# Two groups of the second layer's modulation summed on DVE inside the first layer's up-and-down loop

## The chip, the core and the metric

The kernel runs on one core of a Trainium2 chip. The metric is the device time of one execution in microseconds; the time given is the median of several runs. The engines are PE (TensorE, matmul) with its weight loads PEld, DVE (VectorE), ACT (ScalarE), POOL (GpSimd), and SP, which here only issues DMAs.

## What is computed

The reference is a trunk of two layers for two groups of tokens (128 context tokens and 256 sample tokens, width 1024). Cut to what matters here:

```python
def modulation(cond, w, b):
    m = jax.nn.silu(cond) @ w + b            # w is 1024 x 6144
    return jnp.split(m[..., None, :], 6, axis=-1)

def conv_ffn(h, p):
    gate, up = jnp.split(h @ p['ffn_w_up'], 2, axis=-1)
    gate = dwconv3(gate, p['ffn_conv_w'], p['ffn_conv_b'])
    return (jax.nn.silu(gate) * up) @ p['ffn_w_down']

def trunk_layer(x, mod, p, cache):
    shift1, scale1, gate1, shift2, scale2, gate2 = mod
    h = rms_norm(x, p['norm_g'][0]) * (1.0 + scale1) + shift1
    y, ctx_state = token_mixer(h, p, cache)
    x = x + gate1 * rms_norm(y, p['norm_g'][1])
    h = rms_norm(x, p['norm_g'][2]) * (1.0 + scale2) + shift2
    x = x + gate2 * rms_norm(conv_ffn(h, p), p['norm_g'][3])
    return x, ctx_state
```

Each layer's modulation depends only on the two condition vectors (`c_ctx` and `c`), so any of it can be computed at any time before its use. A layer needs `shift1` and `scale1` first, before its mixer; `gate1`, `shift2` and `scale2` behind the mixer; `gate2` behind the FFN.

## The kernel before

All tokens (3 tiles of 128) are worked on together. A layer has four stages: the token projections and the mixer (its instructions in the order in which a scheduler put them), the output projection with the norms (an order written out by hand, `OUT_ORDER`), the loop of the FFN's up and down products (`for f in range(NF)`, NF = 22, scheduler's order), and the FFN's end with the norms and the first projection of the next layer (by hand, `FFN_ORDER`).

**Weights.** Products of f32 weights are made as three products of rounded parts. A weight tile is loaded raw by a DMA on SP's queue, ACT rounds it to `whi` (L355), DVE takes `wlo = raw - whi` (L356), and L380 to L382 or L1243 to L1245 multiply. One step `f` of the FFN loop does 24 matmuls `gps`, 18 `facc` (down products of step f-1, whose inputs `fah`, `fal` are split from `fc` by ACT and DVE), and 24 `ups`. DVE works between: `fc` (L1257, L1258, L1260 for the convolution and the gate, L1492 for the product with `ups`), `fal` and six `wlo`. `gps` and `ups` share a tag of two PSUM banks, "a".

**Modulation.** The class `Ada(l, g)` computes for layer l the group g, two of the six parts of `modulation` (2048 columns). Its 8 steps k (128 rows of `w` each) load two tiles `araw` of 128x1024 f32 (512 KB each) and make four matmuls with the two condition columns padded to 32 (`cs`), L404, which write four 32-row parts of one bank, `adaps`. In the trace one such matmul is two records, so a step is x8. Then `load_end` loads the bias, `end` adds it on DVE (L426 to L437), `columns` transposes four times on PE (`adat`, L443), and `vec` leaves the result in columns. `hold` lays a part sum aside in `sb` (L413) and frees the bank.

**Where the steps run.** Ada(0,0) at the start. In the mixer of layer 0, as side jobs that the scheduler mixes in, Ada(0,1), Ada(0,2) and the first KO = 3 steps of Ada(1,0); its five others as `A0` to `A4` in `OUT_ORDER`, with `as` (bias), `aT` (transposes) and `vc`. The first KF = 5 steps of Ada(1,1) as `A0` to `A4` in `FFN_ORDER`. In the mixer of layer 1, the last three steps of Ada(1,1) and its end, and all eight of Ada(1,2). The FFN loops hold none of them. `idle` (`W0` and so on in the tables) is eight small bf16 products on PE that compute nothing.

**Names.** `fmps` are the mixer's token projections, `sc` an attention's scores, `ptp` the transposes of its probabilities, `hyt`, `hyP`, `hyR` products of the convolution by FFT, `tma`/`tps` the layer 1 projections and the transposes of the norms. `xn` and `x` are the norm's DVE operations (L752, L736), `tmb` a mixer one (L926).

Of the kernel before, what the change touches and what calls it, by code (L numbers as in the profile page):

```python
# [45 lines left out]
ha2 lv2 L4 ia2 A4 u1 U0 as la2 aT G0 G1 U1 vc  # L46
# [11 lines left out]
L4 k1 A4 lv2 la2 k2 hold  # L58
# [210 lines left out]
def trunk(ctx: ExitStack, tc: tile.TileContext, A, O, offs, depth=DEPTH):  # L269
# [46 lines left out]

    cT = per.tile([128, 8, 2], F32, name="cT")
# [67 lines left out]
    class Ada:  # L385
# [53 lines left out]
        def columns(self, tag="n"):  # L439

            self.tp = bank(tag, "adat").rearrange("p (c j x) -> p j c x", c=4, j=4)
            for c in range(4):
                T.transpose(self.tp[:, :, c], self.sb[:, 128 * c:128 * c + 128], ident)  # L443
# [16 lines left out]
    def ada(a, out, k1=8, part=False):  # L460

        for k in range(a.k0, k1):
            a.load(k)
            a.mm(k, last=k1 - 1)
            if k < k1 - 1:
                yield
        if part:
            a.hold(k1)
        else:
            a.load_end()  # L470
            a.end()
            a.columns()
            a.vec(out)
        yield

# [192 lines left out]
    def retention_tables(lgt, pool=None):  # L668
        with (nullcontext(pool) if pool else tc.tile_pool(name="rp", reuse_waits="tile", bufs=1)) as rp:
            kw = [dict(tag="w15", bufs=11)] * 2 if pool else [dict(tag="lag"), dict(tag="tabt")]  # L670
            lag = rp.tile([128, 384], F32, name="lag", **kw[0])
            nc.sync.dma_start(out=lag, in_=A["lag"])
            return rettab(lgt, lambda: rp.tile([128, 384], F32, name="tabt", **kw[1]), lag)
# [594 lines left out]
    KO, KF = 3, 5  # L1268
# [57 lines left out]
    for l in range(depth):  # L1326
# [4 lines left out]
        with ExitStack() as ph:  # L1331
# [11 lines left out]
            jobs = [ada(ahead.pop((l, 1)) if l else Ada(l, 1), vecs), ada(Ada(l, 2), vecs)]  # L1343
            if l + 1 < depth:
                ahead[l + 1, 0] = Ada(l + 1, 0, "r" * (2 * KO + 5) + "hlhlh" + "r" * 6)
                jobs.append(ada(ahead[l + 1, 0], vecs, KO, True))
# [41 lines left out]
            if l == 0:  # L1388
                mkf = hm.tile([128, 256], F32, tag="hm", name="mkf")
                nc.sync.dma_start(out=mkf, in_=A["mask"])  # L1390
                with tc.issue_after(end.ins):
                    V.tensor_copy(maskb, mkf)
                    lps = load_lp(0)
                    rt = retention_tables(lps[2], mx)
# [32 lines left out]
        with ExitStack() as ph:  # L1427
# [30 lines left out]
            if l + 1 < depth:  # L1458
                a = ahead.pop((l + 1, 0))
                for k in range(8 - KO):  # L1460
                    more[f"L{k}"] = lambda k=k: a.load(k + KO)
                    more[f"A{k}"] = lambda k=k: a.mm(k + KO, "a")
                more["as"] = lambda: (a.load_end(), a.end())
                more["aT"] = lambda: a.columns("a")
                more["vc"] = lambda: a.vec(vecs)
# [3 lines left out]
        with ExitStack() as ph:  # L1469
            fx = ph.enter_context(tc.tile_pool(name="fx", reuse_waits="tile", bufs=1))  # L1470
            act, wd = {}, {}
            for f in range(NF):
# [24 lines left out]
                with late if f == 0 else nullcontext():  # L1497
                    wd[f] = wunit(A["wdn"][l, f], 1024, fx, STAG)
                if f == NF - 1:
                    sqrt_table(c[:, 0:1])  # L1500
                if l + 1 < depth:
                    if f == 4:
# [3 lines left out]
                        rt = retention_tables(lps[2])  # L1506
# [23 lines left out]
            if not last:  # L1530
                a1 = ahead[l + 1, 1] = Ada(l + 1, 1)
                for k in range(KF):
                    more[f"L{k}"] = lambda k=k: a1.load(k)
                    more[f"A{k}"] = lambda k=k: a1.mm(k, "m", KF - 1)
                more["hold"] = lambda: a1.hold(KF)
# [36 lines left out]
```

## Time and profile before

| | us |
|---|---|
| median of 3 runs | 1097.02 (1094.13 to 1098.34) |
| the profiled execution | 1093.04 |
| its span, first to last instruction | 1091.2 |
| PE busy in the span | 1072.9 (98%) |
| DVE busy | 658.5 (60%) |
| ACT busy | 504.6 (46%) |
| POOL busy | 62.0 (6%) |
| granted TensorE clock, mean | 0.999 |

The stages in the span: start and mixer of layer 0 to about 258 us, output projection and norms to 303, FFN loop to 556, its end to 592, mixer of layer 1 to about 760, and the output projection, FFN loop and end of layer 1 to 1091. Busy shares are of one engine; the chain of waits follows the work that ended last back to the start, and the time of its pieces is what the span is made of. A run of matmuls overlaps the next one at its end, so a piece of the chain is a little shorter than the run's own duration.

### The profile page before, as it was taken

The page shows a single profiled execution, that of the slowest core. Times are in us where ns is not written, and L with a number is a line of the kernel's source. Part 1 is how long each engine was busy: PE and PEld are TensorE (multiplying, and loading weights), DVE is VectorE, ACT ScalarE, POOL GpSimd, SP SyncE. Part 2 cuts the span into 40 slices and gives each one's busy share as a digit, 9 for nine tenths or more (in the row PEclk, how much of TensorE's full clock was granted, in tenths as well). Part 3 has the DMA queues.
Part 4 walks back from the last instruction along what each step waited for, and adds up shares of the span by engine and source line. Part 5 has one row for each costly group of instructions (what it writes and reads, how often), then busy time and mean ns, then how long its engine had stood idle before and what let it go on. Part 6 is the DMA issues. An engine that isn't in the chain of part 4 may idle for free.

```text
span 1091.2 us, 15755 instructions
## 1 busy us (share of the span) xinstructions
PE 1072.9 (98%) x5843; PEld 892.9 (82%) x5843; DVE 658.5 (60%) x1479; ACT 504.6 (46%) x1105; POOL 62.0 (6%) x74
## 2 busy tenths in 40 slices
PE   9999999999899999999999999999999999999997
PEld 3496767658699999999987786786889999999996
DVE  6868965466785455455565676637676545554544
ACT  6755535235664343344356534542584333434333
POOL 3210000000300000000002000011020000000000
PEclk9999999999999999999999999999999999999999
DMA  9774345866565433333337615461626433343301
GB/s 348 236 264 167 135 150 198 296 213 249 209 218 160 130 121 120 131 117 121 119 111 267 227 61 169 168 233 43 232 69 213 133 127 116 118 141 127 116 20 58
DMA packets 53018, 176.07 MB, mean 161 GB/s; under 512 B 8618, under 2 KB 10538, under 8 KB 52429
## 3 DMA queue, kind: packets, MB, share of 16 engines
q1 hardware_dynamic: 49229, 171.19, 45.5%
q10 hardware_dynamic: 3712, 3.87, 1.0%
q8 instruction: 46, 0.75, 0.3%
q14 instruction: 31, 0.25, 0.1%
HBM read 169.60 MB, written 5.44 MB: 160 GB/s over the span
## 4 chain that ended last, share of the span: by engine, by line
PE 91%; DVE 5%; ACT 1%; issue 1%; DMA 0%; POOL 0%; DVEq 0%; ACTq 0%; POOLq 0%
PE ups L380 6%; PE gps L380 6%; PE ups L382 6%; PE gps L381 6%; PE gps L382 6%; PE ups L381 6%; PE facc L1243 5%; PE facc L1245 5%; PE facc L1244 5%; PE adaps L404 4%; PE fmps L380 4%; PE fmps L382 4%; PE fmps L381 3%; PE acc L1243 2%; PE acc L1244 2%; PE acc L1245 2%
## 5 line engine op out<-in xcount | busy, mean ns | idle before, releaser
L356 DVE TENSOR_TENSOR wlo<-raw,whi 128x512 fp32r<-128x512 f32 (+2 forms) x388 | 254.3, 686 | 220.8 <-ACT whi L355 220.6
L355 ACT CAST whi<-raw 128x512 fp32r<-128x512 f32 (+2 forms) x388 | 221.0, 610 | 276.8 <-PE gps L381 97.1
L1243 PE MATMUL facc<-whi,fah 128*128 128x512 f32 x264 | 104.5, 396 | 0.0
L1244 PE MATMUL facc<-wlo,fah 128*128 128x512 f32 x264 | 104.0, 394 | 0.0
L1245 PE MATMUL facc<-whi,fal 128*128 128x512 f32 x264 | 104.0, 395 | 0.0
L380 PE MATMUL ups<-hTb,whi 128*128 128x386 f32 (+4 forms) x184 | 61.7, 335 | 0.6 <-ACT hTb L772 0.6
L381 PE MATMUL ups<-hTb,whi 128*128 128x386 f32 (+4 forms) x184 | 61.4, 334 | 0.8 <-POOL hTb L775 0.8
L380 PE MATMUL gps<-hTa,whi 128*128 128x386 f32 (+4 forms) x184 | 61.8, 336 | 0.0
L380 PE MATMUL ups<-hTa,whi 128*128 128x386 f32 (+4 forms) x184 | 61.7, 335 | 0.0
L380 PE MATMUL gps<-hTb,whi 128*128 128x386 f32 (+4 forms) x184 | 61.7, 335 | 0.0
L381 PE MATMUL gps<-hTb,whi 128*128 128x386 f32 (+4 forms) x184 | 61.4, 334 | 0.2 <-POOL hTb L775 0.2
L382 PE MATMUL gps<-hTa,wlo 128*128 128x386 f32 (+4 forms) x184 | 61.5, 334 | 0.0
L382 PE MATMUL ups<-hTb,wlo 128*128 128x386 f32 (+4 forms) x184 | 61.5, 334 | 0.0
L382 PE MATMUL ups<-hTa,wlo 128*128 128x386 f32 (+4 forms) x184 | 61.4, 334 | 0.0
L382 PE MATMUL gps<-hTb,wlo 128*128 128x386 f32 (+4 forms) x184 | 61.3, 333 | 0.0
L381 PE MATMUL gps<-hTa,whi 128*128 128x386 f32 (+4 forms) x184 | 61.3, 333 | 0.0
L381 PE MATMUL ups<-hTa,whi 128*128 128x386 f32 (+4 forms) x184 | 61.3, 333 | 0.0
L1245 PEld LDWEIGHTS facc<-whi,fal 128*128 128x128 f32 x264 | 49.6, 188 | 12.1 <-DVE fal L356 0.3
L404 PE MATMUL adaps<-araw,cs 128*32 128x512 f32 x384 | 59.4, 602 | 0.0
L1243 PEld LDWEIGHTS facc<-whi,fah 128*128 128x128 f32 x264 | 49.6, 188 | 10.2 <-ACT fah L355 0.3
L1244 PEld LDWEIGHTS facc<-wlo,fah 128*128 128x128 f32 x264 | 49.6, 188 | 10.0
L1259 ACT ACTIVATE fth<-fc 128x386 f32<-128x386 f32 x44 | 23.2, 528 | 55.1 <-DVE fc L1258 55.0
(367 smaller groups left out, 2319.6 us busy)
## 6 DMA issues: line engine op xcount, KB each, us to landing
araw<-in_ada_dram SPq DMA_DIRECT2D x96, 512.0 KB, 5.1
raw<-in_wup_dram SPq DMA_DIRECT2D x88, 512.0 KB, 3.5
raw<-in_wdn_dram SPq DMA_DIRECT2D x44, 512.0 KB, 3.8
raw<-in_win_dram SPq DMA_DIRECT2D x30, 512.0 KB, 4.3
raw<-in_wout_dram SPq DMA_DIRECT2D x16, 512.0 KB, 5.1
gg<-gd SPq DMA_DIRECT2D x8, 512.0 KB, 6.1
raw<-in_wta_dram SPq DMA_DIRECT2D x8, 416.0 KB, 3.2
x<-in_x_dram SPq DMA_DIRECT2D x6, 512.0 KB
```

The source lines that it names most:

```text
L355: S.copy(hi, src)
L356: (eng or V).tensor_tensor(out=lo, in0=src, in1=hi, op=ALU.subtract)
L380: T.matmul(out, ah, bh, start=start, stop=False)
L381: T.matmul(out, ah, bl, start=False, stop=False)
L382: T.matmul(out, al, bh, start=False, stop=stop)
L404: T.matmul(self.ps[32 * j:32 * j + 32, :], cs[:, k, :], rows[j // 2][:, 512 * (j % 2):512 * (j % 2) + 512], start=(k == self.k0), stop=(k ...
L1243: T.matmul(acc[t][h], ah[:, cs_], wh_[:, hs], start=first, stop=False)
L1244: T.matmul(acc[t][h], ah[:, cs_], wl_[:, hs], start=False, stop=False)
L1245: T.matmul(acc[t][h], al[:, cs_], wh_[:, hs], start=False, stop=last)
L1259: S.activation(out=th, in_=c, func=ACTF.Tanh)
```

## The change

The groups 0 and 2 of layer 1 no longer go over `adaps`. A class `AdaV` loads the same tiles into `avr` (two buffers) and lets DVE multiply each by the condition's value of its row and add it up: `acc` is 128 x 2 conditions x 2048 f32, and each tile takes two DVE operations of 128x1024, `tensor_scalar` for k = 0 and `scalar_tensor_tensor` behind it. When all 16 tiles are in, eight matmuls with a column of ones sum the 128 partitions into a bank of tag "a" (`avps`), and `end`, `columns` and `vec` follow as before. This runs in the FFN loop of layer 0: every step f but 0, 4 and 5 asks twice for the next tile, until both groups are through. So DVE gets 8 operations of `tensor_scalar` and 56 of `scalar_tensor_tensor`, PE 2 x 8 matmuls with ones and 2 x 4 transposes, and SP 32 DMAs of 512 KB in that loop.

Group 1 of layer 1 keeps `adaps`: four steps in `OUT_ORDER`, in place of the five of group 0 (the fifth place becomes `W0`, and `as`, `aT`, `vc` are gone), four in `FFN_ORDER` in place of five (the fifth becomes `W0`; the bias is added there), and only its transposes in the mixer of layer 1. The mixer of layer 0 has no step of layer 1 any more. Of 16 steps that are gone from PE, 3 stood in the mixer of layer 0, 1 in the output stage, 1 in the FFN's end and 11 in the mixer of layer 1. The retention's tables (`lag`, `tab`), which DVE makes at f = 4, lie in the `avr` buffers now.

```diff
 OUT_ORDER:
-ha2 lv2 L4 ia2 A4 u1 U0 as la2 aT G0 G1 U1 vc
+ha2 lv2 ia2 W0 u1 U0 hold la2  G0 G1 U1 
 FFN_ORDER:
-L4 k1 A4 lv2 la2 k2 hold
+ k1 W0 lv2 la2 k2 as
...
+    one = per.tile([128, 34], F32, name="one")
+    V.memset(one, 0.0)
+    V.memset(one[:, 1:2], 1.0)
...
+    def ada_last(a, out):
+        a.columns()
+        a.vec(out)
+        yield
+
+    class AdaV(Ada):
...
+        def rows(self, out):
+            acc = self.pool.tile([128, 2, 2, 1024], F32, tag="avc", name="avc")
+            for k in range(8):
+                for c in range(2):
+                    raw = self.pool.tile([128, 1024], F32, tag="avr", name="avr", bufs=2)
+                    nc.sync.dma_start(out=raw, in_=A["ada"][self.l, 2 * self.g + c, k])
+                    for v in range(2):
+                        sc = cs[:, k, v:v + 1]
+                        if k == 0:
+                            V.tensor_scalar(acc[:, v, c], raw, sc, None, ALU.mult)
+                        else:
+                            V.scalar_tensor_tensor(out=acc[:, v, c], in0=raw, scalar=sc, in1=acc[:, v, c], op0=ALU.mult, op1=ALU.add)
+                    yield
+            self.load_end()
+            ps = self.ps = bank("a", "avps")
+            for v in range(2):
+                for j in range(4):
+                    T.matmul(ps[32 * j:32 * j + 32, :], one[:, 1 - v:33 - v], acc[:, v, j // 2, 512 * (j % 2):512 * (j % 2) + 512],
+                             start=(v == 0), stop=(v == 1))
+            self.end()
+            self.columns(ps)
+            self.vec(out)
+            yield
...
-    KO, KF = 3, 5
+    KO = 4
...
-            jobs = [ada(ahead.pop((l, 1)) if l else Ada(l, 1), vecs), ada(Ada(l, 2), vecs)]
-            if l + 1 < depth:
-                ahead[l + 1, 0] = Ada(l + 1, 0, "r" * (2 * KO + 5) + "hlhlh" + "r" * 6)
-                jobs.append(ada(ahead[l + 1, 0], vecs, KO, True))
+            jobs = [ada_last(ahead.pop((l, 1)), vecs)] if l else [ada(Ada(l, 1), vecs), ada(Ada(l, 2), vecs)]
...
-                a = ahead.pop((l + 1, 0))
-                for k in range(8 - KO):
-                    more[f"L{k}"] = lambda k=k: a.load(k + KO)
-                    more[f"A{k}"] = lambda k=k: a.mm(k + KO, "a")
-                more["as"] = lambda: (a.load_end(), a.end())
-                more["aT"] = lambda: a.columns("a")
-                more["vc"] = lambda: a.vec(vecs)
+                a = ahead[l + 1, 1] = Ada(l + 1, 1, "rrrhlhlh" + "r" * 8)
+                for k in range(KO):
+                    more[f"L{k}"] = lambda k=k: a.load(k)
+                    more[f"A{k}"] = lambda k=k: a.mm(k, "a", KO - 1)
+                more["hold"] = lambda: a.hold(KO)
...
+            avc = tc.tile_pool(name="av", reuse_waits="tile", bufs=1, side="right")
+            av = avc.__enter__()
+            nexts = iter([])
+            if l + 1 < depth:
+                nexts = (s for g in (0, 2) for s in AdaV(l + 1, g, av).rows(vecs))
             for f in range(NF):
...
                     wd[f] = wunit(A["wdn"][l, f], 1024, fx, STAG)
+                if f not in (0, 4, 5):
+                    next(nexts, None)
+                    next(nexts, None)
...
-                        rt = retention_tables(lps[2])
+                        rt = retention_tables(lps[2], av, tag="avr", bufs=2)
+            run(nexts)
+            avc.__exit__(None, None, None)
...
-                a1 = ahead[l + 1, 1] = Ada(l + 1, 1)
-                for k in range(KF):
-                    more[f"L{k}"] = lambda k=k: a1.load(k)
-                    more[f"A{k}"] = lambda k=k: a1.mm(k, "m", KF - 1)
-                more["hold"] = lambda: a1.hold(KF)
+                a1 = ahead[l + 1, 1]
+                for k in range(8 - KO):
+                    more[f"L{k}"] = lambda k=k: a1.load(k + KO)
+                    more[f"A{k}"] = lambda k=k: a1.mm(k + KO, "m")
+                more["as"] = lambda: (a1.load_end(), a1.end())
+                more["W0"] = idle
```

The lines of the changed kernel are moved: L356 is L359 there, L380 to L382 are L383 to L385, L404 is L407, L443 is L446, L885 is L925, L1018 and L1020 are L1058 and L1060, L1257, L1258 and L1260 are L1297, L1298 and L1300, and L1492 is L1533. The DVE sums are L503 and L505, the matmuls with ones L511.

**DVE in the FFN loop.** Before, one step of the loop, from the product with `ups` to the next one:

```order
L1492 TENSOR_TENSOR fc<-ups,fc 128x386
L356 TENSOR_TENSOR wlo<-raw,whi 128x512 x2
L356 TENSOR_TENSOR fal<-fc,fah 128x386
L356 TENSOR_TENSOR wlo<-raw,whi 128x512
L1257 SCALAR_TENSOR_TENSOR fc<-gps,ffh,fc 128x385
L356 TENSOR_TENSOR wlo<-raw,whi 128x512
L1258 SCALAR_TENSOR_TENSOR fc<-gps,ffh,fc 128x385
L1260 SCALAR_TENSOR_TENSOR fc<-fth,fc 128x386
L356 TENSOR_TENSOR wlo<-raw,whi 128x512 x2
```

Now, a step in which the second group is summed, from behind the product with `ups` to before the next one:

```order
L505 SCALAR_TENSOR_TENSOR avc<-avr,cs,avc 128x1024
L359 TENSOR_TENSOR fal<-fc,fah 128x386
L359 TENSOR_TENSOR wlo<-raw,whi 128x512 x2
L505 SCALAR_TENSOR_TENSOR avc<-avr,cs,avc 128x1024
L1297 SCALAR_TENSOR_TENSOR fc<-gps,ffh,fc 128x385
L359 TENSOR_TENSOR wlo<-raw,whi 128x512
L1298 SCALAR_TENSOR_TENSOR fc<-gps,ffh,fc 128x385
L359 TENSOR_TENSOR wlo<-raw,whi 128x512
L505 SCALAR_TENSOR_TENSOR avc<-avr,cs,avc 128x1024
L1300 SCALAR_TENSOR_TENSOR fc<-fth,fc 128x386
L505 SCALAR_TENSOR_TENSOR avc<-avr,cs,avc 128x1024 x2
L359 TENSOR_TENSOR wlo<-raw,whi 128x512
```

Five sums stand between the loop's own operations, here one of them ahead of `fal`. In the whole loop the steps hold 1, 4, 5, 2, 3, 5, 4, 5, 3, then none in three, then 9 (the second group's start, four of them `tensor_scalar`), 5, 5, 5, 5 and 3.

**PE where the first group ends.** After the `ups` of a step, ahead of the next `gps`:

```order
L385 MATMUL ups<-hTb,wlo 128x386
L511 MATMUL avps<-avc,one 32x512 x8
L383 MATMUL gps<-hTa,whi 128x386
L384 MATMUL gps<-hTa,whi 128x386
L385 MATMUL gps<-hTa,wlo 128x386
L383 MATMUL gps<-hTa,whi 128x386
L384 MATMUL gps<-hTa,whi 128x386
L385 MATMUL gps<-hTa,wlo 128x386
L383 MATMUL gps<-hTa,whi 128x386
L384 MATMUL gps<-hTa,whi 128x386
L446 MATMUL avps<-cst_79,avs 128x128 x4
L385 MATMUL gps<-hTa,wlo 128x386
```

The matmuls with ones and the transposes stand in PE's row of weight products, eight `gps` apart; the second group's are 14 apart.

**PE in the mixer of layer 1.** Before, behind a block of attention scores:

```order
L1018 MATMUL sc<-gqk 128x384
L1020 LDWEIGHTS identb
L1020 MATMUL sc<-maskb,identb 128x128
L404 MATMUL adaps<-araw,cs 32x512 x3
L380 MATMUL fmps<-hTa,whi 128x386
L381 MATMUL fmps<-hTa,whi 128x386
L382 MATMUL fmps<-hTa,wlo 128x386
```

Now, at the same place:

```order
L1058 MATMUL sc<-gqk 128x384
L1060 LDWEIGHTS identb
L1060 MATMUL sc<-maskb,identb 128x128
L385 MATMUL fmps<-hTb,wlo 128x386
L383 MATMUL fmps<-hTb,whi 128x386
L384 MATMUL fmps<-hTb,whi 128x386
L385 MATMUL fmps<-hTb,wlo 128x386
```

Until the transposes `ptp` of these scores' probabilities there stood `adaps` x3, 24 `fmps`, `adaps` x4 and 2 `fmps`; now 26 `fmps`.

## Rows read from the trace of the kernel before

**Rows 1.** The page: span, busy time by engine, chain that ended last.

```profile
span 1091.2 us, 15755 instructions
PE 1072.9 (98%) x5843; PEld 892.9 (82%) x5843; DVE 658.5 (60%) x1479; ACT 504.6 (46%) x1105; POOL 62.0 (6%) x74
PE 91%; DVE 5%; ACT 1%; issue 1%; DMA 0%; POOL 0%; DVEq 0%; ACTq 0%; POOLq 0%
```

**Rows 2.** Busy time by stretch: length, engines, granted clock, DMA share, GB/s.

```profile
306.00:556.00 250.00, 250.00 (x1309) 235.15 (x1308) 138.18 (x245) 102.72 (x191) 0.33 (x2) 1.00 0.42 134
592.00:720.00 128.00, 128.00 (x751) 97.63 (x750) 79.01 (x207) 60.46 (x162) 5.09 (x7) 1.00 0.48 173
650.00:700.00 50.00, 50.00 (x324) 34.70 (x323) 34.28 (x93) 23.69 (x67) 0.00 (x0) 1.00 0.50 169
403.16:415.84 12.68, 12.68 (x68) 11.88 (x67) 6.45 (x11) 4.94 (x10) 0.00 (x0) 1.00 0.38 124
```

**Rows 3.** Chain of waits, 612 to 716 us (mixer, layer 1): shares, one piece.

```profile
by line: PE fmps L380 15.4%; PE fmps L382 14.5%; PE fmps L381 14.1%; PE adaps L404 12.3%; PE pv L890 8.4%; PE ptp L885 6.9%; PE sc L1018 6.5%; PE sc L976 6.4%; PE uqps L965 5.0%; DMA raw<-in_win_dram 4.7%; PE uvps L958 1.9%; PE ukps L952 1.
673.59 0.99 PE adaps L404 x6
```

**Rows 4.** PE's own row: start, duration, line, operation, records.

```profile
720.14 1.07 PE L404 MATMUL adaps<-araw,cs 128*32 128x512 f32 x8
680.42 0.82 PE L885 MATMUL ptp<-cst,P 128*128 128x128 f32 x6
205.43 1.92 PE L404 MATMUL adaps<-araw,cs 128*32 128x512 f32 x16
796.12 0.61 PE L1278 MATMUL wps<-identb 128*128 128x128 bf16 x8
407.68 0.39 PE L1245 MATMUL facc<-whi,fal 128*128 128x512 f32 x1
```

**Rows 5.** Chain of waits, 212 to 224 us (end of layer 0's mixer): shares.

```profile
by line: PE adaps L404 47.6%; PE fmps L382 14.6%; PE fmps L380 10.3%; PE fmps L381 10.2%; PE hyR L1062 8.7%; PE hyP L1086 5.2%; PE hyP L1085 5.2%; PE hyI L1063 3.6%
```

**Rows 6.** Chain of waits, pieces in the output stage and in the FFN's end.

```profile
292.95 0.99 PE adaps L404 x8
296.88 0.46 PE adat L443 x4
...
583.93 0.99 PE adaps L404 x8
```

**Rows 7.** What PE waited for, 600 to 800 us: total, times, longest.

```profile
PE hyF L1104 <- POOL Y L1078: 0.4, 1, 0.4
PE adat L443 <- DVE sb L434: 0.3, 1, 0.3
```

**Rows 8.** DVE's own row in one step of layer 0's FFN loop [idle before].

```profile
403.16 0.56 DVE L1492 TENSOR_TENSOR fc<-ups,fc 128x386 f32<-128x386 f32 x1 [0.75 <-PE ups L382]
...
404.85 0.56 DVE L356 TENSOR_TENSOR fal<-fc,fah 128x386 fp32r<-128x386 f32 x1
...
410.90 0.56 DVE L1260 SCALAR_TENSOR_TENSOR fc<-fth,fc 128x386 f32<-128x386 f32 x1 [0.66 <-ACT fth L1259]
413.82 1.29 DVE L356 TENSOR_TENSOR wlo<-raw,whi 128x512 fp32r<-128x512 f32 x2 [2.36 <-ACT whi L355]
415.84 0.56 DVE L1492 TENSOR_TENSOR fc<-ups,fc 128x386 f32<-128x386 f32 x1 [0.73 <-PE ups L382]
```

**Rows 9.** Durations of DVE operations by line: ns min/median/max, first and last start, forms.

```profile
L926 DVE SCALAR_TENSOR_TENSOR tmb<-tmb,ry,lm x12: 346/416/481, 81.0 to 613.8; 128x128 f32<-128x128 f32 x6, 128x256 f32<-128x256 f32 x6
L736 DVE SCALAR_TENSOR_TENSOR x<-yn,rz,x x24: 741/748/1680, 267.1 to 1087.3; 128x512 f32<-128x512 f32 x24
L752 DVE TENSOR_SCALAR xn<-x,rz x12: 472/488/1385, 32.9 to 801.6; 128x512 f32<-128x512 f32 x12
```

**Rows 10.** The page's DMA issues: KB each, median us from issue to landing.

```profile
araw<-in_ada_dram SPq DMA_DIRECT2D x96, 512.0 KB, 5.1
raw<-in_wup_dram SPq DMA_DIRECT2D x88, 512.0 KB, 3.5
```

More of the change, by code (lines that the diff above doesn't have):

```diff
@@ L439, in columns @@
         def columns(self, tag="n"):
-            self.tp = bank(tag, "adat").rearrange("p (c j x) -> p j c x", c=4, j=4)
+            self.tp = (bank(tag, "adat") if isinstance(tag, str) else tag).rearrange("p (c j x) -> p j c x", c=4, j=4)
             for c in range(4):
@@ L474, in ada, with __init__, sums @@
         yield
+    def ada_last(a, out):
[3 more added lines that the diff above has]
+    class AdaV(Ada):
+        def __init__(self, l, g, pool):
+            super().__init__(l, g)
+            self.pool = pool
+        def sums(self):
+            return self.pool.tile([128, 512], F32, tag="avs", name="avs")
+        def rows(self, out):
[21 more added lines that the diff above has]
+            yield
     def gate_rows(sb, j0, slot):
@@ L666, in filter_steps, with retention_tables @@
                 st[f"s{l}{t}"] = lambda l=l, b=t: save(l, b)
[L668 to L673, printed above, removed]
+    def retention_tables(lgt, pool, **kw):
+        lag = pool.tile([128, 384], F32, name="lag", **kw)
+        nc.sync.dma_start(out=lag, in_=A["lag"])
+        return rettab(lgt, lambda: pool.tile([128, 384], F32, name="tabt", **kw), lag)
     def half_tiles(name, pads):
@@ L1393, in trunk @@
                     lps = load_lp(0)
-                    rt = retention_tables(lps[2], mx)
+                    rt = retention_tables(lps[2], mx, tag="w15", bufs=11)
             get, fh, lgt = lps
```

## The prediction

> **What bounds the kernel now.** The page comes first. PE is busy 98% of the span, and the chain that ended last is 91% PE and 5% DVE [rows 1]. So what is taken off PE's row can be time, and what is put on another engine is free only as long as PE never waits for it. The second view is busy time by stretch [rows 2]: in layer 0's FFN loop PE is busy in 250.00 of 250.00 us, DVE in 138.18 and POOL in nearly nothing; in the mixer of layer 1 PE is busy in all of 128 us and DVE in 79. DVE has its room in the loop, and PE has none anywhere. The third is the chain inside the stages that lose work: how many of its pieces are modulation matmuls, which says what their removal is worth there and not only how long they run. The last is the list of what PE waited for: in the 200 us that hold layer 1's mixer, two waits of 0.7 us together [rows 7].
>
> **What is removed.** In the mixer of layer 1, modulation matmuls are 12.3% of the chain between 612 and 716 us [rows 3], 12.8 us for ten of the eleven steps that go. The eleventh stands at 720.14 with 1.07 us [rows 4], some 1.0 of it its own. With the group's transposes (0.46 by the ones of the output stage [rows 6]) and the wait ahead of them (0.3 [rows 7], they move to the mixer's beginning) this is 14.5 us. At the end of layer 0's mixer they are 47.6% of 12 us [rows 5]: 5.7 us for three steps, more than three times 0.99, because they are cut into five runs and a run of one or two matmuls costs as much as one of four. Bounds are 2.9 (whole runs) and 5.7; I take 5.7, since the chain holds each of the five. In the output stage a run of 0.99 and the transposes of 0.46 go, and the filler W0 comes [rows 6], a run of eight bf16 products of 0.61, of which about 0.5 is its own [rows 4]: 0.95 us. In the FFN's end 0.99 goes and 0.5 comes: 0.5 us. Removed in all: 14.5 + 5.7 + 0.95 + 0.5 = 21.65 us.
>
> **What is added on PE.** Two runs of matmuls with ones. Each has the form of 16 modulation records, for which one row shows 1.92 us [rows 4], and each brings transposes of 0.46: 2 x 1.92 + 2 x 0.46 = 4.75 us. They stand in the FFN loop, where PE has no gap to hide them. Balance on PE: 16.9 us less.
>
> **What is added on DVE.** No row shows a two-tensor operation of 1024 columns. The nearest are of 128, 256 and 512 columns: 346, 481 and 748 ns [rows 9]. They lie on a line, 0.134 us for each 128 columns, which gives 0.346 + 7 x 0.134 = 1.28 us for 1024; behind another operation it costs a little less, 1.2 us, since two `wlo` take 1.29 together [rows 8]. The operation with one tensor takes 472 ns for 512 columns [rows 9]; for 1024 that is between 0.74, if its fixed part is like the other's, and 0.94. So 56 x 1.2 + 8 x 0.74 = 73 us for the two groups, against 250 - 138 = 112 us in which DVE is idle in the loop [rows 2]. In sum it fits. By step it is tight: a step of the loop takes PE 12.68 us, with 6.45 us of DVE's own work in it [rows 2], 6.1 when its operations stand close. Steps with five sums make 6.1 + 6.0 = 12.1 at best and 6.45 + 6.4 = 12.85 at worst, against 12.68. Seven steps have five. The step that starts the second group has four single-tensor ones as well and the first group's end: 6.1 + 6.0 + 3.0 + 0.5 = 15.6, 2.9 us too many.
>
> What is queued behind DVE, and who waits for it? `fal` is the tight one. It ends at 404.85 + 0.56 = 405.41 [rows 8], and the first product that needs it starts at 407.68 [rows 4]: 2.3 us to spare. The `wlo` of the weights are made a good part of a step or more ahead. A sum put ahead of `fal` fits where it is, as the gap between the product with `ups` and `fal` holds two `wlo` now. So DVE may be up to 2.3 us late before PE stands still, but then each further us is lost in full.
>
> The tiles can make it late: there are two buffers, and one tile goes through a buffer in two sums and a transfer, 2.4 + 5.1 = 7.5 us, the transfer by the median of the same tiles in other stages [rows 10]. That gives 2 x 12.68 / 7.5 = 3.4 tiles in a step, and two and a half are needed; but a tile is asked for on SP's queue only when its buffer is free, and the weight loads of the next steps (3.5 us [rows 10]) stand behind that. The loop's DMAs move 134 GB/s [rows 2]; 16.8 MB more over some 210 us are 80 GB/s, not much beside the 169 GB/s of the mixer [rows 2]. I put PE's stalls for a late DVE at 5 us: 3 where the second group starts, 1 where the retention's tables are made in the step after other sums, 1 elsewhere. The bounds are 0 (all of it is covered by the 2.3 us) and 22 (below).
>
> **What the fillers covered.** In the mixers the removed runs also filled time in which PE would have waited. Behind one block of scores PE had a run of modulation at 673.59 [rows 3], and the transposes that need the probabilities started at 680.42 [rows 4], 6.8 us later and without a wait, so the softmax needs at most that. Now 26 matmuls of 0.18 us stand there, 4.7 us. The loss at such a place is between 0 and 2.1 us, and the mixer of layer 1 has four or five of them, with the convolution's inputs: 0 to 10 us. I take 2.5, as the scheduler put other projections into the holes.
>
> **The sum.** -16.9 + 2.5 + 5 = -9.4 us. Against the profiled execution, 1093.04, this is 1083.6. The median of the runs before is 3.98 higher, 1097.02, so the forecast is 1087.6, rounded 1088.
>
> **Rival 1: the mixers give it back as waits.** A PE that is busy in every us may be busy with matmuls that are stretched over time it has. For it: between 650 and 700 us PE is busy in 50.00 of 50, but its weight loads only in 34.70, where the FFN loop has 235 of 250 [rows 2]. Then PE has slack there, and the runs that go leave waits for softmax and DVE behind. Against it: the chain passes through the removed runs themselves [rows 3, 5], and next to no wait is on record there [rows 7]. By its price the lost cover is the full 10 us in place of 2.5: 1088 + 7.5 = 1095. The Trainium skill, page "Perfetto Trace Analysis", section "Identifying the Most-Contended Engine", holds that matmul busy time is a poor measure of how close a kernel is to its limit and that the share of weight loads is the better one. By that rule the mixer of layer 1 is at 69% and not at 100%, and this rival gains; the chain of this trace speaks against it, so I leave it at a small chance.
>
> **Rival 2, slower: DVE becomes the bound of the loop.** DVE takes its instructions in order. Each step now holds waits that no sum can fill where the order puts none: 0.75 for `ups` and 0.66 for ACT's gate [rows 8]. The wait of 2.36 for the rounded down weights [rows 8] is filled. If the two recur and a tile lands 0.9 us late in each step, a heavy step takes 12.1 + 1.4 + 0.9 = 14.4 us in place of 12.68. DVE's lateness then adds up from step to step, and after two steps the 2.3 us are used up. The nine steps with four or five sums give 15 us, the second group's start and the tables 4.5, in all 20; where the four steps with two or three suffer as well, 13 steps give 22. Then -16.9 + 2.5 + 20 = +5.6, 1102.6 against the median, and up to 1107 with tiles that hold the weight loads up. It decides from 14.4 us of stalls on: 1.1 us for each of 13 steps. For it: heavy steps have 0.6 us of room at best. Against it: in the order the sums stand in the gaps in which DVE waited, and light steps (2, 3, none) come between heavy ones.
>
> **How the numbers follow.** Forecast 0.65, rival 1 0.17, rival 2 0.18. A measurement of this kernel can tell about 0.5%, 5.5 us, from no change: faster is below 1091.5, slower above 1102.5. The forecast lies 3.5 us inside faster, and its stalls can be larger: 0.55 faster, 0.10 the same. Rival 1 gives 0.03 and 0.14; rival 2 gives 0.03 the same and 0.15 slower. In all 0.58, 0.27, 0.15. The range runs from the bare balance on PE, 1097.02 - 16.9 = 1080, to a little above rival 2's time, 1104.
>
> **What would show it.** In the profile after: PE has some 5 us of waits for DVE in layer 0's FFN loop, most in the step that starts the second group, and the loop is about 10 us longer than its 250; a two-tensor sum takes 1.2 to 1.3 us; a run of matmuls with ones 1.9; the mixer of layer 1 is shorter by 12, that of layer 0 by 5. Rival 1 shows as waits of PE for DVE or ACT ahead of `ptp` and `hyt` in the mixers, 10 us in all. Rival 2 shows as steps of 14 us in the loop and waits of `facc` for `fal`, or of ACT's casts for weight DMAs. The prediction is wrong if a sum of 1024 columns takes clearly more than 1.4 us, if tiles land much later than 5.1 us, or if `avps` holds its bank so long that `ups` waits.

## The result

The changed kernel takes 1084.53 us (median, 1083.77 to 1086.07) against 1096.78 for the kernel before: a ratio of 0.9892, 95% interval 0.987 to 0.9915. Beside later experiments, on other chips, the same two kernels gave 0.9907 (0.9889 to 0.9926), 0.9914 (0.9891 to 0.9937) and 0.9912 (0.9892 to 0.9933). So it is about 1% faster, 9 to 12 us, where 9 were forecast. The changed kernel's median differs by up to 3.5 us between these comparisons, and the profiled execution of the kernel before (1093.04) lies 4 us below its median; the granted clock differs by execution at two places, shown at the end, and that is about as large. The stages of the traces are steadier than the medians, and the argument goes by them.

The page of the changed kernel, its span, busy times and the chain by engine, answers to [rows 1]:

```profile
span 1082.9 us, 15620 instructions
PE 1059.6 (98%) x5763; PEld 894.1 (83%) x5763; DVE 727.2 (67%) x1544; ACT 504.3 (47%) x1106; POOL 61.5 (6%) x74
PE 86%; DVE 8%; DMA 2%; ACT 2%; issue 1%; POOL 0%; ACTq 0%; DVEq 0%; SPq 0%; POOLq 0%
```

PE is busy 13.3 us less, DVE 68.7 us more, and PE's share of the span has stayed: the time came off the engine that bounds the kernel. New is 2% of DMA in the chain.

The traces can be cut at points where PE's own row shows the same instruction in both kernels: the first projection of layer 0 (`tma`), the last product of its output projection (`acc`), the last of the two projections in the FFN's end, the last `fmps` of layer 1's mixer, and the last down product. Worked out from the starts of these instructions, the stages changed by:

| stage (us) | before | after | difference | forecast |
|---|---|---|---|---|
| start | 47.17 | 48.40 | +1.2 | 0 |
| mixer and output products of layer 0 | 231.64 | 226.08 | -5.6 | -5.7 |
| its norms, FFN loop and FFN's end | 330.02 | 338.24 | +8.2 | -0.95 + 4.75 + 5 - 0.5 = +8.3 |
| mixer of layer 1 | 126.55 | 113.42 | -13.1 | -14.5 and part of 2.5 |
| rest of layer 1 | 348.57 | 349.46 | +0.9 | 0 |

The stretches that answer to [rows 2], the loop of layer 0 and the mixer of layer 1 (length, then busy time of PE, PEld, DVE, ACT, POOL, granted clock, DMA share, GB/s):

```profile
306.00:556.00 250.00, 249.68 (x1309) 230.69 (x1310) 203.59 (x311) 98.41 (x183) 0.00 (x0) 0.99 0.62 195
592.00:720.00 128.00, 125.28 (x734) 105.58 (x733) 83.66 (x213) 65.98 (x174) 6.43 (x9) 1.00 0.32 102
```

DVE has 203.59 us of work in the 250 us in which it had 138.18, and PE is idle for a third of a microsecond; the one large wait, shown below, ends just ahead of this stretch. What PE waited for between 300 and 560 us, and between 600 and 740 (total, times, longest):

```profile
PE facc L1283 <- ACT fah L358: 2.7, 1, 2.7
PE facc L1285 <- DVE fal L359: 0.2, 1, 0.2
...
PE ukps L992 <- ACT ckvT L975: 1.0, 1, 1.0
PE uvps L998 <- ACT mv L999: 0.7, 1, 0.7
PE uvps L998 <- ACT mk L987: 0.3, 1, 0.3
PE hyt L1095 <- DVE fo L1091: 0.3, 1, 0.3
PE pv L930 <- ACT PT L926: 0.3, 1, 0.3
```

In the mixer of layer 1, 2.6 us of waits stand where there were 0.3 of one [rows 7]: that is time which the removed runs had covered.

**The one large wait.** It is where the first sum of all stands. DVE's own row at f = 1, then ACT's and PE's (start, duration, [idle before]):

```profile
303.27 0.75 DVE L503 TENSOR_SCALAR avc<-avr,cs 128x1024 f32<-128x1024 f32 x1 [4.05 <-DMA avr<-in_ada_dram]
303.94 0.56 DVE L1300 SCALAR_TENSOR_TENSOR fc<-fth,fc 128x386 f32<-128x386 f32 x1
304.41 0.61 DVE L1297 SCALAR_TENSOR_TENSOR fc<-gps,ffh,fc 128x385 f32<-128x385 f32 x1
304.94 0.55 DVE L1533 TENSOR_TENSOR fc<-ups,fc 128x386 f32<-128x386 f32 x1
...
305.53 0.51 ACT L358 CAST fah<-fc 128x386 fp32r<-128x386 f32 x1 [3.09 <-DVE fc L1533]
...
306.09 0.79 PE L1283 MATMUL facc<-whi,fah 128*128 128x512 f32 x1 [2.72 <-ACT fah L358]
```

DVE stands still for 4.05 us for a tile, with the gate of f = 0, the product with `ups`, and thereby `fah` and the first down product queued behind the sum that needs the tile. The chain of waits shows where the tile had been, start and duration, and the list of SP's waits (total, times, longest) what had held the queue ahead of it:

```profile
295.79 0.33 SPq L363
296.21 6.97 DMA avr<-in_ada_dram
303.27 0.75 DVE avc L503
...
SPq L363 <- DVE wlo L359: 18.1, 5, 14.8
```

It could be issued only at 296.21, behind weight loads on SP's queue that had themselves waited up to 14.8 us for a `wlo` to free their buffer, and took 6.97 us to land in place of the 5.1 of [rows 10], while the DMA engines were full (share 1.01 and 414 GB/s between 302 and 304 us, below). And the wait had a second price. Stretches of 2 us from 302 us on:

```profile
302.00:304.00 2.00, 1.38 (x8) 1.05 (x6) 0.73 (x2) 0.44 (x1) 0.00 (x0) 1.00 1.01 414
304.00:306.00 2.00, 0.00 (x0) 0.00 (x0) 2.00 (x6) 0.47 (x2) 0.00 (x0) 0.92 0.73 299
306.00:308.00 2.00, 1.91 (x5) 1.52 (x6) 2.00 (x5) 1.99 (x5) 0.00 (x0) 0.50 0.29 29
308.00:310.00 2.00, 2.00 (x8) 1.63 (x7) 2.00 (x4) 0.14 (x1) 0.00 (x0) 0.73 0.69 246
```

After PE's pause the granted clock was 0.50, 1.2 GHz, and the 18 down products took 5.8 us (306.09 to 311.89) where they took 4.4 before. Wait and slow clock are 4.1 us, most of the 5 that the forecast had put down for a late DVE, at a place it did not name.

**What the added work costs.** The first run of matmuls with ones and its transposes on PE, and the two kinds of sum on DVE (min/median/max ns):

```profile
440.60 1.92 PE L511 MATMUL avps<-avc,one 128*32 128x512 f32 x16
443.97 0.60 PE L446 MATMUL avps<-cst,avs 128*128 128x128 f32 x4
...
L505 DVE SCALAR_TENSOR_TENSOR avc<-avr,cs,avc x56: 1274/1282/1291, 311.3 to 516.1; 128x1024 f32<-128x1024 f32 x56
L503 DVE TENSOR_SCALAR avc<-avr,cs x8: 745/750/753, 303.3 to 445.7; 128x1024 f32<-128x1024 f32 x8
```

All three are as forecast: 1.92, 1.28 and 0.75 us. By the starts of the product with `ups` in each step of the loop, the distance to the kernel before grows by 2.48 us at the first group's run and by 2.49 at the second's, so 4.97 us for both.

### The profile page after: what moved, and what is told of

Read it like the earlier page. It is cut to its first block, busy times and chain, and to the rows that moved or that the text cites. A ratio compares the mean times of both kernels' runs of the same rounds, so it can differ in the third digit from the quotient of the medians.

```text
span 1082.9 us, 15620 instructions
## 1 busy us (share of the span) xinstructions
PE 1059.6 (98%) x5763; PEld 894.1 (83%) x5763; DVE 727.2 (67%) x1544; ACT 504.3 (47%) x1106; POOL 61.5 (6%) x74
## 4 chain that ended last, share of the span: by engine, by line
PE 86%; DVE 8%; DMA 2%; ACT 2%; issue 1%; POOL 0%; ACTq 0%; DVEq 0%; SPq 0%; POOLq 0%
PE ups L383 5%; PE ups L385 5%; PE ups L384 5%; PE gps L383 5%; PE facc L1283 5%; PE facc L1285 5%; PE gps L385 5%; PE gps L384 5%; PE facc L1284 5%; PE fmps L383 4%; PE fmps L385 4%; PE fmps L384 4%; PE adaps L407 2%; PE acc L1283 2%; PE acc L1284 2%; PE acc L1285 2%
## 5 line engine op out<-in xcount | busy, mean ns | idle before, releaser
L359 DVE TENSOR_TENSOR wlo<-raw,whi 128x512 fp32r<-128x512 f32 (+2 forms) x388 | 254.4, 686 | 169.0 <-ACT whi L358 168.5
L505 DVE SCALAR_TENSOR_TENSOR avc<-avr,cs,avc 128x1024 f32<-128x1024 f32 x56 | 70.3, 1282 | 0.3 <-DMA avr<-in_ada_dram 0.2
L383 PE MATMUL gps<-hTa,whi 128*128 128x386 f32 (+4 forms) x184 | 62.5, 340 | 0.0
L383 PE MATMUL ups<-hTb,whi 128*128 128x386 f32 (+4 forms) x184 | 61.7, 335 | 0.6 <-ACT hTb L812 0.6
L385 PE MATMUL gps<-hTa,wlo 128*128 128x386 f32 (+4 forms) x184 | 62.0, 337 | 0.0
L383 PE MATMUL gps<-hTb,whi 128*128 128x386 f32 (+4 forms) x184 | 61.7, 335 | 0.0
L383 PE MATMUL ups<-hTa,whi 128*128 128x386 f32 (+4 forms) x184 | 61.7, 335 | 0.0
L385 PE MATMUL ups<-hTb,wlo 128*128 128x386 f32 (+4 forms) x184 | 61.5, 334 | 0.0
L385 PE MATMUL gps<-hTb,wlo 128*128 128x386 f32 (+4 forms) x184 | 61.4, 334 | 0.0
L385 PE MATMUL ups<-hTa,wlo 128*128 128x386 f32 (+4 forms) x184 | 61.4, 334 | 0.0
L1285 PEld LDWEIGHTS facc<-whi,fal 128*128 128x128 f32 x264 | 50.0, 189 | 13.1 <-DVE fal L359 1.3
L1284 PEld LDWEIGHTS facc<-wlo,fah 128*128 128x128 f32 x264 | 50.0, 190 | 10.1
```

Source lines behind the costliest of these rows:

```text
L359: (eng or V).tensor_tensor(out=lo, in0=src, in1=hi, op=ALU.subtract)
L383: T.matmul(out, ah, bh, start=start, stop=False)
L385: T.matmul(out, al, bh, start=False, stop=stop)
L505: V.scalar_tensor_tensor(out=acc[:, v, c], in0=raw, scalar=sc, in1=acc[:, v, c], op0=ALU.mult, op1=ALU.add)
L1284: T.matmul(acc[t][h], ah[:, cs_], wl_[:, hs], start=False, stop=False)
L1285: T.matmul(acc[t][h], al[:, cs_], wh_[:, hs], start=False, stop=last)
```

## The experiments

**Whether the wait stays.** The changed kernel was measured again beside each set of others.

> The changed kernel once more, as the neighbour of the next three. 1084.5 us again, and in its trace the same two things: PE waits about 2.7 us for the first down product of layer 0's FFN loop (DVE's first sum waits for its tile, and the gate, fal and fah stand behind it), and nothing over 0.3 us elsewhere in the loop. If that wait is chance in the arrival of one tile, it will differ from 2.7 by a microsecond or more, or be gone.

1087.68 us, 3 us more than expected. Of the difference to the first trace of this kernel, 3.1 us lie in the rest of layer 1, behind a pause of PE that the last section shows. The loop has one wait:

```profile
PE facc L1283 <- ACT fah L358: 2.4, 1, 2.4
```

In two more sets,

> The changed kernel as the neighbour of the next three: 1084 to 1088 us, as on two chips before. By stages of its trace: the wait of some 2.5 us for the first down product of layer 0's FFN loop again, with a granted clock of half behind it.

> The changed kernel as the neighbour of the next: 1084 to 1088 us.

it took 1086.86 and 1087.98 us, with that wait at 2.5 and 2.9 us. So the wait is part of the program, not of one execution. The clock behind it fell to half in the first three of the four traces and stayed at 1.00 in the last; the stage from the output product to the FFN's end cost 8.2, 7.6, 7.2 and, without the slow clock, 6.3 us more than before.

**The first sum behind the gate.**

> The changed kernel with one rule more for its order: the first sums of the first group come on DVE after the product of the gate with ups of step f = 1. Transfers stand where they stood. Theory (the loop's loss is a queue behind one late tile): DVE makes the gate at once, the wait of 2.7 us goes, and with it the slow clock behind it, which stretched the 18 down products from 4.2 to 5.8 us; so 4.3 us less, 1080.2. Rival (the loss is DVE's load, and the first tile is only where it shows): the same sums still have to be made, eight of them now in one step, and the wait moves to a later fal; 1083 to 1085.

```diff
-                            V.tensor_scalar(acc[:, v, c], raw, sc, None, ALU.mult)
+                            with tc.issue_after(self.after) if self.after else nullcontext():
+                                V.tensor_scalar(acc[:, v, c], raw, sc, None, ALU.mult)
...
-                V.tensor_tensor(out=c, in0=pu[:, 0:TP], in1=c, op=ALU.mult)
+                gated = V.tensor_tensor(out=c, in0=pu[:, 0:TP], in1=c, op=ALU.mult)
...
+                if f == 1 and l + 1 < depth:
+                    av0.after = gated.ins
```

1082.72 us against 1087.68 for its neighbour. The stage from the output product to the FFN's end gained less than that: it costs 6.4 us more than before, where the neighbour's costs 7.6. Of the rest of the difference, 0.8 us lie in the start and 3.1 in the rest of layer 1, and 0.8 are lost in the mixer of layer 0, all at places that the edit does not touch. What PE waited for in the loop, where the longest wait is, what stood ahead of it on DVE and ACT, and a piece of the chain of waits:

```profile
PE facc L1284 <- ACT fah L358: 1.6, 2, 1.4
PE facc L1286 <- DVE fal L359: 0.3, 1, 0.3
...
366.34 0.50 PE L1284 MATMUL facc<-whi,fah 128*128 128x512 f32 x1 [1.44 <-ACT fah L358]
...
363.73 0.55 DVE L1535 TENSOR_TENSOR fc<-ups,fc 128x386 f32<-128x386 f32 x1
364.74 1.14 ACT L358 CAST whi<-raw 128x512 fp32r<-128x512 f32 x2 [3.09 <-DMA raw<-in_wdn_dram]
365.78 0.51 ACT L358 CAST fah<-fc 128x386 fp32r<-128x386 f32 x1
...
359.62 0.61 DVE wlo L359
360.25 4.47 DMA raw<-in_wdn_dram
```

The wait at f = 1 is gone with its slow clock, as the theory said: right behind that place PE is 4.2 us ahead of the neighbour. Over the next steps 3.0 us of it are lost again, 1.9 of them in waits, as the rival said that it would be, but by another way than a late product on DVE. The product with `ups` ends at 364.28, in time; ACT stands still for 3.09 us for a tile of a down weight, and `fah` is queued behind the rounding of that tile. The tile's transfer was issued at 360.25, when a `wlo` of DVE had freed a buffer, and took 4.47 us, where the median in this loop was 3.4 before. In these steps stand eight sums in one step, the retention's tables and then up to five sums a step; that they are what made the `wlo` late is argued and not shown. Theory and rival were right in part.

**How much of it is the sums.**

> The changed kernel with only the first two of each group's 16 tiles loaded and summed (8 of the 64 sums, 4 of the 32 transfers; the matmuls with ones and all behind them stay). The modulation of layer 1 is wrong by what is left out. Theory: the other 56 sums and 28 transfers cost next to nothing, since DVE's lateness stays inside the room ahead of fal; the first wait stays. 1083.5 to 1084.5. Rival (DVE and the transfers load the loop): 3 to 5 us less, 1080 to 1081.5.

```diff
                 for c in range(2):
+                    if k:
+                        yield
+                        continue
                     raw = self.pool.tile([128, 1024], F32, tag="avr", name="avr", bufs=2)
```

1084.29 us, with 1079.74 to 1087.69 the widest spread of all. By the median, 3.4 us below the neighbour's, the rival is nearer, by the trace the theory: the stage costs 7.7 us more than before, and 7.6 in the neighbour. That 56 sums and 28 transfers fewer change next to nothing in it shows that the loop's loss in the neighbour, beside the matmuls with ones, was the first wait with its slow clock. In the first trace of the changed kernel 0.8 us stand elsewhere in the loop.

**Where DVE's limit is.**

> The changed kernel with 28 sums of 128x1024 more: of every pair of tiles but the first, one is added twice (the modulation of layer 1 is wrong by that). A step with five sums has seven or eight, 6.1 + 7.5 x 1.2 = 15.1 us of DVE work in a step of 12.68. Theory (DVE becomes the bound of the loop as soon as a step's work is over 12.7 us): 2.4 us late in each of nine steps, some of it made good in the light steps and by the 2.3 us ahead of fal; 12 to 18 us more, 1097 to 1103. Rival (DVE has room, because its idle time in the loop is 46 us in all and 28 sums take 34): under 5 us more.

```diff
+                            if c == 0:
+                                V.scalar_tensor_tensor(out=acc[:, v, c], in0=raw, scalar=sc, in1=acc[:, v, c], op0=ALU.mult, op1=ALU.add)
```

1086.25 us, by the median no slower than the neighbour's 1087.68. The loop's stretch, to be read against 203.59 us of DVE in the changed kernel, and its waits:

```profile
306.00:556.00 250.00, 246.92 (x1294) 228.13 (x1295) 235.88 (x339) 98.37 (x182) 0.00 (x0) 0.99 0.57 189
...
PE facc L1285 <- ACT fah L358: 2.5, 1, 2.5
PE gps L383 <- DVE fc L1535: 1.4, 2, 1.1
PE avps L446 <- ACT avs L440: 0.4, 1, 0.4
```

DVE is busy in 235.88 of 250 us, and the stage costs 9.9 us more than before, 2.3 more than its neighbour's. The loss stands at two places, where the matmuls with ones of a group take a bank of tag "a": the distance to the kernel before grows there by 3.4 and 4.4 us and not by 2.5, as `gps` waits for DVE's product with `ups`, which comes late. So 28 sums more cost 2.3 us, as the rival said (under 5), and not the 12 to 18 of the theory. The theory fell by its premise: the scheduler did not put seven or eight sums into a step, but mostly five or six, and filled steps that had been empty. What has to be ready in its step, `fc` and `fal`, must not be late; the `wlo` are made ahead and give way.

**What the removed runs are worth, one stage at a time.**

> The kernel before, without the three steps of the second layer's group 0 in the mixer of layer 0 (the modulation of layer 1 is wrong by these rows); all else stays. Theory (each run of one to four modulation matmuls takes about a microsecond of PE, and five runs go): 5.7 us less. By whole steps, three times 0.99, it would be 3 us less. Rival (the runs filled waits of the convolution, so that waits come in their place): under 2 us less.

```diff
-                jobs.append(ada(ahead[l + 1, 0], vecs, KO, True))
+                ahead[l + 1, 0].k0 = KO
```

1091.75 us, a ratio of 0.9943 (0.9931 to 0.9956), 6 us less. In its trace the stage is 3.9 us shorter, with a lower clock in one stretch of it, while PE was busy throughout:

```profile
164.00:172.00 8.00, 8.00 (x41) 6.87 (x41) 3.67 (x12) 3.13 (x10) 0.00 (x0) 0.79 0.17 48
```

By the first `hyt` behind this stretch the kernel was 1.6 us later than the kernel before; with that taken out it is 5.5 us. The runs, not the whole steps, were the unit: three steps cut into five runs cost five times 1.1 us.

> The kernel before, with two of the eleven modulation steps in the mixer of layer 1 left (the last of each group; the modulation of layer 1 is wrong by the other nine); ends and transposes stay. Theory (the runs lie on PE's path, and the scheduler fills what they covered with other projections): 13 runs become 2 or 3, 10.5 to 11.5 us less, of which up to 2.5 come back as waits of PE; so 8 to 11 us less. Rival (they filled the waits for the softmax and for the convolution): no more than 4 us less, with some 7 us of waits for DVE or ACT ahead of ptp, pv and hyt.

```diff
     def ada(a, out, k1=8, part=False):
+        if a.l == 1 and k1 == 8:
+            a.k0 = 7
         for k in range(a.k0, k1):
```

1085.37 us, a ratio of 0.9881 (0.9864 to 0.9897). By the medians that is 12.4 us less, more than expected; by the trace the mixer of layer 1 is 10.3 us shorter, with 1.3 us of waits ahead of `uvps` and `hyt`. The rival, that the mixers give it back, is out: of the 10.5 to 11.5 us removed, 10.3 are time.

**The start.**

> The changed kernel with its two small memsets for the column of ones put behind the one that PE's first filler matmuls wait for; they are 0.15 us long and stand ahead of it in the changed kernel. In the five traces of kernels with the early memsets the projections of layer 0 start 0.9 to 2.8 us later than in the three without them, because the granted clock rises later in the start. Theory (that 0.04 us shift at the start decides it): the projections start at 47.2 us as in the kernel before, and the kernel is 1 to 2 us faster than its neighbour. Rival (something else in the start, or chance): they start at 48 to 50 us again.

1085.54 us against 1086.86, no difference beyond the interval. The projections start at 48.43 us with the late memsets, and at 47.24 in the neighbour with the early ones. Over all fourteen traces they start 0 to 2.8 us later than in the kernel before, whichever the order. The theory falls; the start differs by execution.

**Two edits for the loop.**

> The rule of the second kernel above (first sums behind the gate of f = 1) and one tile in place of two asked for in each of the steps f = 1, 2 and 3, so that six sums and not fourteen come before the retention's tables. Theory (what is left of the loop's loss in that kernel, waits of 1.4 and 0.5 us behind steps with eight sums and the tables, is DVE's lateness by too much work in three steps in a row): these waits go, the loop takes its 250 us and the two runs with ones, 5 us more and not 8 or 6.5, and the kernel is 3 to 4 us faster than its neighbour. Rival: the same lateness comes later, in the steps of the first group that are now pushed together, and nothing is gained on the second kernel above.

Beside the rule for the first sum, shown above, the edit is:

```diff
                 if f not in (0, 4, 5):
-                    next(nexts, None)
-                    next(nexts, None)
+                    for _ in range(1 if f < 4 else 2):
+                        next(nexts, None)
```

1085.31 us against 1086.86: not the 3 to 4 us. The stage costs 10.1 us more than before. In this execution DVE waited 1.0 us for a tile (0.3 in the next kernel) and ACT up to 6.0 us for a weight load (4.5 there), just where steps with five sums begin, and PE lost 2.4 us in waits for `fah` and `fal` at three steps. Besides, the second group's sums ended only behind the last step, and its matmuls came in the FFN's end. There the distance to the kernel before grew by 4.5 us (3.9 in the next kernel), where the changed kernel pays 2.5 for them in the loop and gains 0.55 in the end. In both executions the granted clock fell there behind a wait of PE of 2.0 us (0.61 over 4 us in this one, 0.60 in the next); in the changed kernel's end it stayed at 1.00.

> The two edits together: 4 to 6 us faster than its neighbour, about 1080, if both theories hold; each edit's part is seen in its own stage of the trace.

The late memsets and the light start together: 1084.02 us, 2.8 less than the neighbour and not the 4 to 6 expected; the intervals of the two overlap. PE and DVE have the same order in the loop as in the kernel above, yet the trace has not one wait of PE in it, and the stage costs 5.75 us more than before. So a full order of DVE leaves the loop to the arrival of single transfers: beside the matmuls with ones the same order lost 0.7 us in one execution and 4.3 in another, 2.4 of it in waits.

> As the kernel with both edits, and three tiles in place of two asked for in the steps f = 9 to 12, so that the second group's sums end where they end in the changed kernel and its matmuls with ones stand inside the loop, ahead of gps, and no longer behind the last step, where they came in the FFN's end. Theory: no wait at the loop's start, no clock at half behind it, and 2.5 us for each of the two runs with ones and their transposes: the loop and the FFN's end together cost 4.5 to 5.5 us more than before, against 7.0 to 8.3 in the changed kernel; 2 to 4 us faster than its neighbour. Rival (the loop's loss moves with the arrival of single transfers, and no order takes it away): the loop and the FFN's end still cost 7 us or more, and there is no difference beyond the interval.

Against the kernel above:

```diff
-                    for _ in range(1 if f < 4 else 2):
+                    for _ in range(1 if f < 4 else 3 if 8 < f < 13 else 2):
                         next(nexts, None)
```

1082.77 us against 1087.98 for the changed kernel beside it; against the kernel before 0.9872 (0.9854 to 0.9891). The stage costs 3.2 us more than before, less than the 4.5 to 5.5 expected, which had left out the 1.1 us gained at its beginning. The loop's stretch, without a wait of PE:

```profile
306.00:556.00 250.00, 250.00 (x1325) 232.26 (x1324) 204.49 (x313) 99.79 (x185) 0.32 (x2) 1.00 0.63 198
```

Same sums, same tiles, same 204 us of DVE: 3 to 5 us less in the stage than in the changed kernel. The first sum no longer stands ahead of the gate, which alone took the first wait away above, and the retention's tables come behind six sums and no longer behind twelve. What the second is worth by itself is not shown: there is one trace of this kernel, and the one with the same beginning of the loop lost 0.7 and 4.3 us in two. An earlier transfer of the first tile, which would go at the first wait directly, was not tried. This is the fastest of the kernels with the whole computation by its trace (span 1077.1); by the median it is level with the one that had the first edit alone.

## Why the prediction was right, and where it was not

**The terms on PE held.** Mixer of layer 0: 5.7 us forecast from its share of the chain [rows 5], 5.6 measured, and 5.5 in the experiment that removed these steps alone; the bound of 2.9 by whole steps was too low. (Over the eleven traces with this change the stage gained 4.5 to 5.7.) Mixer of layer 1: 14.5 removed [rows 3, 4], 13.1 gained in this trace and in the ten others with this change within 0.1 us, so by this sum 1.4 net was lost cover. Waits of 2.6 us are on record. The term was 2.5 for both mixers. Output stage: 0.95 forecast, 1.1 measured by the start of f = 1's `gps` (301.14 before, 295.71 after, 4.34 of the difference from earlier stages). FFN's end: 0.5 and 0.55. Two runs with ones: 4.75 and 4.97, a run and its transposes costing 2.48 and not 2.38 on PE.

**The price of a sum held.** The line through 128, 256 and 512 columns [rows 9] gave 1.28 us for 1024; it is 1.282. The single-tensor one lies at the lower end of its bounds, 0.75.

**The stalls of the loop: the size held, the step behind it failed.** The forecast put 5 us down for a late DVE: 3 where the second group starts, 1 at the tables, 1 elsewhere. In the trace it is 4.9 (9.85 for the loop less 4.97): 2.7 of wait and 1.4 of slow clock at the first sum, 0.2 of another wait, and some 0.6 spread. At the second group's start PE did not wait at all, though 9 sums stand in that step; DVE came to the product with `ups` 1.3 us later than PE's own delay explains (457.12 against 453.92 before, with PE 1.95 us behind), within the 2.3 us of room. What the prediction overlooked is the first tile. It had reckoned how often two buffers can be filled in steady state, from a transfer of 5.1 us [rows 10], and not when the first transfer can begin and what stands behind the first sum. For the slow clock it had no term. That the sum came out right with the wrong place is luck, not foresight.

**The last term of the sum did not show in the first comparison.** The forecast added 3.98 us, by which the median of the kernel before lay above its profiled execution. The changed kernel's profiled execution (1084.69) lies at its median there (1084.53), and 1087.6 was 3 us too high; in the three later sets the medians are 1086.86 to 1087.98, 9.4 to 9.7 below the kernel before, where the balance was 9.4. That is nearer than the terms themselves came: in this trace the three stages that had terms changed by 10.5 us together, and start and rest gave 2.1 back.

**Rival 2 had its mechanism only in part.** Waits for `fah` and `fal`, and ACT's waits for weight tiles ahead of them, came in two of the experiments, as its sign said. But the step's work did not decide: with 32 us more on DVE the stage cost 2.3 us more, and at two places only. The reckoning by step (12.1 to 12.85 us of work against 12.68) took the order as fixed in each step and the room ahead of `fal` as the only one; the `wlo` made ahead are a larger one, as long as none is so late that it holds back the next weight's transfer.

**Rival 1 is out.** In the mixer of layer 1 weight loads filled 97.63 of 128 us [rows 2], 76%, and all but 1.4 of the 14.5 us on PE's path was time nevertheless. The Trainium skill, page "Perfetto Trace Analysis", section "Identifying the Most-Contended Engine", counts the share of weight loads among the better measures of how close a kernel is to its limit; for the question what a removed run is worth, the chain through the runs decided here, and the lower share of weight loads did not show slack.

## What to carry to other kernels

Where the chain of waits passes through a run of small matmuls, its removal is worth the run, not its matmuls: here runs of one to four cost about a microsecond each, so first ask into how many pieces a scheduler has cut the work. Work moved to an engine with idle time is nearly free as long as the engine has its timely outputs done. What must be looked at is the first instruction of the moved work: the engine kept its order here and held the gate back behind it, and a single late tile cost 4.1 of the 4.9 us that the move lost beyond its own matmuls. A rule that orders the first use behind the urgent work took that wait away; what then remained went with the arrival of single tiles, and was 0.1 to 4.3 us by execution and order.

## What the runs showed of the hardware

The granted clock after a pause of PE is a matter of the execution. In the output stage of layer 1 PE stands still for 2.0 us in all fourteen traces, waiting for the norms. The same place in the kernel before, where the clock held, and in the changed kernel, measured again:

```profile
802.00:804.00 2.00, 0.87 (x9) 0.90 (x9) 1.11 (x2) 2.00 (x6) 1.78 (x2) 1.00 0.00 0
804.00:808.00 4.00, 3.78 (x33) 3.58 (x32) 1.24 (x4) 2.94 (x8) 2.14 (x3) 1.00 0.00 0
...
792.00:794.00 2.00, 0.19 (x2) 0.22 (x3) 1.60 (x3) 1.83 (x5) 1.57 (x2) 1.00 0.00 0
794.00:798.00 4.00, 4.00 (x24) 4.00 (x23) 1.37 (x4) 2.98 (x8) 2.14 (x3) 0.58 0.02 4
798.00:802.00 4.00, 4.00 (x20) 4.00 (x20) 2.30 (x3) 3.97 (x9) 2.16 (x2) 0.50 0.01 2
```

Over the fourteen traces the rest of layer 1 behind its mixer takes as long as in the kernel before within 0.3 us (four traces, its own among them), or 0.9 (two), 2.4 (three) or 4.0 us (five) longer, with a granted clock of 0.50, 1.2 GHz, behind the pause for none of the time, for a few us or for some 10.

The start varies by 2.8 us. The same seven filler matmuls in the kernel before and in the one with few sums (the profile's row of the granted clock has 1.00 in both, so the durations must tell it):

```profile
8.90 1.67 PE L1297 MATMUL wps<-wz 128*128 128x512 bf16 x7
...
10.62 3.19 PE L1340 MATMUL wps<-wz 128*128 128x512 bf16 x7
```

They take nearly twice as long, as at half the clock, and the projections start 2.8 us later. Not all of the start is this: in the kernel with the first sum behind the gate the fillers take 1.67 us and the projections start 0.85 later. Start and pause together are about the spread of the medians, and one profiled execution may hold any of it. The mean granted clock of every run points the same way: over 42 runs of the kernel before beside these experiments, the two at 0.999 took 1093.5 us in the mean and the nineteen at 0.994 took 1098.4.

The start agrees with the Trainium skill, page "TensorE: Matmul & The Clock Gate", section "Part 1: The HAM clock gate (the "warmup" mystery)", which says that the slow stretch at a kernel's start varies from run to run; that the same holds for a pause in the middle of a kernel is what these traces add.
